# Output stage of a transformer layer: raw weights requested in the gate's stage, other first PSUM banks, form buffers held for six jobs, high parts of a set ahead of its low parts

## The chip, the cores and the metric

The kernel runs on one core of a Trainium2 chip. TensorE (PE in the profile) multiplies, VectorE (DVE) and ScalarE (ACT) do the elementwise work, GpSimd (POOL) and SyncE (SP) issue DMA transfers between the chip's main memory and the core's SBUF. Matmul results land in PSUM, which has eight banks of 128 x 512 fp32. The metric is the device time of one execution, in microseconds (us).

## The reference

One layer with 512 tokens and a width of 2048, everything in fp32:

```python
def reference(x, ...):                       # kind 0 for the one layer here
    h = rms_norm(x, norm_g[i, 0])
    y = gla_mixer(h, gla_w_in, gla_w_a2, gla_b_a, gla_g_norm, gla_w_out)
    x = x + y
    x = x + swiglu(rms_norm(x, norm_g[i, 1]), ffn_w_gu[i], ffn_w_down[i])
    return x

def gla_mixer(h, w_in, w_a2, b_a, g_norm, w_out):
    q, k, v, r, a_lr = split(h @ w_in)
    ...                                      # gated linear attention in chunks of 64 tokens -> o
    o = rms_norm(o, g_norm) * silu(r)        # the gate
    return o @ w_out                         # the output product

def swiglu(h, w_gu, w_down):
    g, u = jnp.split(h @ w_gu, 2, axis=-1)
    return (silu(g) * u) @ w_down
```

## The kernel before, in words

**fp32 by halves.** TensorE multiplies in a reduced form of fp32 (fp32r). Each operand is split in a high part (a cast on ACT) and a low part (the operand less its high part, on DVE), and a product is three matmuls: high x high, high x low, low x high. So each raw weight block that comes by DMA passes ACT (`hi`, L121 or L697) and DVE (`lo`, L122 or L698) before PE can use it. A ring of three pairs (`wp`, bufs=3) holds the parts.

**The gate's stage.** The last of the products with w_in are four groups (`group(X, KT)`), one for each head of the gate; each multiplies 16 blocks and leaves its sums in four banks named `acc`. The raw blocks come by SP (L108) into two buffers. `gate(h, banks)` (L575) then takes a group's banks: four products acc x R1 (L579) into `t`, a Silu on ACT (L583), a product with the attention's output (L584), and after that its pieces in steps, spread over the work that follows by a queue. `put` splits each piece into high and low parts (`split_into`, L559) and stores them through POOL to a DRAM tensor gF; `load_form` (L573) loads them back on SP as "forms", the left operands of the next products.

**The output stage and the FFN in jobs.** Each big product is done by a scheme of seven products of blocks in place of eight. A "group" is 28 jobs: seven phases (`PHASES`) of four chunks. Groups 0 and 1 are the two halves of the product with w_out, the groups from 2 on are w_gu's and w_down's. A job is twelve 128x512 matmuls (`run_job`, L1064 to L1066). Ahead of job m, `add_stage(m + 3)` subtracts or adds raw blocks on DVE (L688) where the phase wants a sum of blocks, and `split_stage` makes the parts (L697, L698) up to two jobs ahead. `load` (L676) asks for raw blocks on SP. The sums of the phases stand in pairs of banks x, y and z. The first pairs are made in `first_banks`, out of the same eight banks that acc (five) and the attention's `mis` (three) held before.

**What is hung on job numbers.** `at(m, fn)` runs fn behind job m's matmuls in program order. After each phase of groups 0 and 1, `take_out` moves the banks into SBUF pieces u, v, s, w (L883 copies, L886 to L898 adds), adds the residual x, and `finish` squares a finished piece on ACT for the second norm (L875) and stores it to x1d (L876, POOL). In group 0, `make_forms` turns the finished pieces (transposes, L766) and makes the FFN's forms in four steps, each in one job: `one` (high and low parts times the gain, L565 on ACT and L566 on DVE, and a scaled copy, L795), `two` (store of `hh` and `hl`, and sums on DVE, L789), `three` (parts of the sums, L824 and L825), `four` (store of the rest). The stores go to xF by POOL (L803). There are four such sets, and `hh`, `hl` and `hs` have one buffer each. Group 1's forms are made by a class `Direct` straight into place. `second_norm` (L743) computes the inverse root of the row sums: DVE, then two table functions on ACT (L162, L163), then a Newton step on DVE (L164 to L167).

The program's order on each engine is the order in which the code issues it; nothing is rescheduled. What sets the order around the change is the job numbers in `at`, the place of the calls of `load`, and the steps of `gate`.

Of the kernel before, what the change touches and what calls it, by code (L numbers as in the profile page):

```python
# [14 lines left out]
P = 128  # L15
# [21 lines left out]
def f32(ap):  # L37
    return ap.bitcast(F32)
# [3 lines left out]
def trunk_kernel(ctx: ExitStack, tc: tile.TileContext, x, xT, cst, masks, wa2r, w_in, w_out, w_gu, w_down, out):  # L42
# [516 lines left out]

    def split_into(hi, lo, src, g=None):  # L560
        if g is None:
            nc.scalar.copy(hi, src)  # L562
            nc.vector.tensor_sub(lo, src, f32(hi))
        else:
            nc.scalar.activation(hi, src, AF.Copy, scale=g)  # L565
            nc.vector.scalar_tensor_tensor(lo, src, g, f32(hi), ALU.mult, ALU.subtract)  # L566
# [69 lines left out]
    for h in range(3):  # L636
        queue.append(gate(h, banks))
        tick()
        banks = group(X, KT, after=early_load) if h == 2 else group(X, KT)
    while queue:  # L640
        tick()
    for f in ("e0", "e1", "e2", "e3"):
        load_form(gF, f, 2)
    x1d = dram.tile([P, 4, D], F32, name="x1d")

# [63 lines left out]
    for blk in range(3):  # L709
        for j in range(4):  # L710
            load(0, blk, j)
# [13 lines left out]
    first_banks = {q: [bank(f"q{pr}{i}") for i in range(2)] for q, pr in (("z", 0), ("y", 1), ("x", 2))}  # L725
# [18 lines left out]
    def second_norm():  # L744
        z = sp.tile([P, S], F32, tag="u1", name="z")
        c = z[:, 16:20]
# [4 lines left out]
        rsqrt(c, D, r2c, (z[:, 0:4], z[:, 8:12]))  # L751

    at(first_of[G0, 1] + 2, second_norm)
# [43 lines left out]
    def make_forms(dst, c, i, tiles, m, banks, g=None):  # L797
# [7 lines left out]
        def one():  # L805
# [4 lines left out]
            if g is None:  # L810
                split_into(hi[:, 0:2], lo[:, 0:2], a1)
                split_into(hi[:, 2], lo[:, 2], a2[:, 1])
            else:
                for k, src in enumerate((a1[:, 0], a1[:, 1], a2[:, 1])):
                    split_into(hi[:, k], lo[:, k], src, g[min(k, 1)])
            copy_scaled(sm[:, 0], a2[:, 0], g)
# [17 lines left out]
    class Direct:  # L834
# [16 lines left out]
        def pure(self, f, i):  # L851
            t, (a1, a2), g = self.place(f), self.a[i], self.gain(i)
            src, gg = {"e0": (a1[:, 0], g[0]), "e3": (a1[:, 1], g[1]), "l2": (a2[:, 1], g[1])}[f]
            split_into(t[:, 0, i], t[:, 1, i], src, gg)
# [7 lines left out]
        def part(self, f, i):  # L862
            t = self.place(f)
            split_into(t[:, 0, i], t[:, 1, i], self.sm[i][:, ("e1", "e2", "l0", "l1").index(f)])


    def take_out(g, ph, XYZ, keep):
# [6 lines left out]
        def finish(tt, nb, t, junk):  # L874
            nc.scalar.activation(junk, t, AF.Square, accum_out=ssq2[:, 4 * tt + nb : 4 * tt + nb + 1])  # L875
            nc.gpsimd.dma_start(x1d[:, tt, nb * G : (nb + 1) * G], t)  # L876

        for i in range(2):
# [6 lines left out]
            elif ph == 3:  # L885
                nc.vector.tensor_add(keep["u", i], keep["u", i], y)  # L886
                finish(i, 2 * p + 1, keep["u", i], y)
            elif ph == 4:
                nc.vector.tensor_add(keep["v", i], keep["v", i], b)
                finish(2 + i, 2 * p + 1, keep["v", i], y)  # L890
                t = keep["x", i] = piece()
                nc.sync.dma_start(t, x_at(2 + i, 2 * p))
            elif ph == 5:
                nc.vector.tensor_add(keep["s", i], keep["s", i], z)
                finish(i, 2 * p, keep["s", i], z)
            else:
                t = keep["w", i] = sp.tile([P, S], F32, tag=f"v{i}", name="w")
                nc.vector.tensor_add(t, keep["x", i], b)  # L898
                finish(2 + i, 2 * p, t, b)
        if ph == 4:  # L900
            tiles = [keep[k, i] for k in "uv" for i in range(2)]
            c = 2 * p + 1
            if p == 0:
                g_ = [[g2[:, 4 * c + k : 4 * c + k + 1] for k in (i, 2 + i)] for i in range(2)]
                at(m0 + 21, lambda: make_forms(xF, c, 0, tiles, m0 + 21, tb_pair(), g_[0]))
                at(m0 + 22, lambda: make_forms(xF, c, 1, tiles, m0 + 25, pair(1), g_[1]))
            else:
                d = Direct(c)
                at(m0 + 21, lambda: d.turn(tiles, 0, tb_pair()))
                at(m0 + 22, lambda: (d.turn(tiles, 1, pair(1)), d.pure("e0", 0)))  # L910
                at(m0 + 23, lambda: (d.pure("e0", 1), d.sums(0)))
                at(m0 + 24, lambda: [d.part(f, 0) for f in ("e1", "e2", "l0", "l1")])
                at(m0 + 25, lambda: d.sums(1))
                at(m0 + 26, lambda: [d.part(f, 1) for f in ("e1", "e2", "l0", "l1")])
# [231 lines left out]
```

## Time and profile before

| | us |
|---|---|
| median of 3 runs | 2108.28 (2108.11 to 2109.48) |
| the profiled execution | 2110.94 |
| its span in the profile | 2109.1 |
| PE busy | 2073.3 (98%) |
| DVE busy | 1604.6 (76%) |
| ACT busy | 938.1 (44%) |
| POOL busy | 311.4 (15%) |

PE's mean granted clock over the span is 0.994. The output stage lies between about 630 and 857 us of the span: group 0 from 637.9 to 720.6, group 1 to about 818, then the first w_gu group. Each row of a timeline has a start, a length, engine, line, operation, output and inputs; in brackets stands the time for which the engine was idle just before, and what released it.

### The profile page before, as it was taken

What the parts mean: (1) busy time and instruction counts of PE and PEld (TensorE: products, weight loads), DVE (VectorE), ACT (ScalarE), POOL (GpSimd) and SP (SyncE); (2) the same over time, 40 slices, a digit from 0 to 9 for tenths busy, and PEclk for the clock granted to TensorE, in tenths of its full rate; (3) what the DMA queues carried; (4) which work ended last, traced back from release to release, by engine and by line L of the source; (5) the groups of instructions that cost most, each with busy time, mean ns of one, the idle gap of its engine ahead of it and who ended that gap; (6) DMA issues with size and microseconds to landing.
All of it is one profiled execution on the core that took longest, in us unless ns stands there. A gap on an engine that the chain in (4) does not pass through costs nothing.

```text
span 2109.1 us, 24558 instructions
## 1 busy us (share of the span) xinstructions
PE 2073.3 (98%) x9314; PEld 1714.5 (81%) x9314; DVE 1604.6 (76%) x1778; ACT 938.1 (44%) x1165; POOL 311.4 (15%) x315
## 2 busy tenths in 40 slices
PE   9999999999998989999999999999999999999999
PEld 7887888888877767788888888888888888888887
DVE  7857475755448778788788788788798787888887
ACT  6343433333334445554454454454455454333333
POOL 5315151422111120010010010010010010000000
PEclk9999999999999999999999999999999999999999
DMA  6222222225586866444644644644645776675642
GB/s 209 80 81 71 70 83 77 71 85 165 161 307 200 310 201 258 141 138 146 185 136 139 185 141 134 186 148 125 195 146 164 249 274 239 219 254 192 233 145 100
DMA packets 161333, 350.22 MB, mean 166 GB/s; under 512 B 14400, under 2 KB 30912, under 8 KB 161216
## 3 DMA queue, kind: packets, MB, share of 16 engines
q1 hardware_dynamic: 136704, 274.76, 40.4%
q0 software_dynamic: 21440, 71.84, 10.0%
q10 hardware_dynamic: 3072, 2.06, 0.3%
q8 instruction: 73, 1.20, 0.2%
q14 instruction: 44, 0.36, 0.1%
HBM read 279.93 MB, written 68.68 MB: 165 GB/s over the span
## 4 chain that ended last, share of the span: by engine, by line
PE 86%; issue 6%; DVE 4%; POOL 2%; DMA 1%; ACT 1%; SPq 0%; POOLq 0%; ACTq 0%; DVEq 0%
PE bank L1066 20%; PE bank L1065 20%; PE bank L1064 20%; PE acc L134 7%; PE acc L133 7%; PE acc L135 7%; PE mis L427 2%; PE bank L766 1%; DVE lo L698 1%; PE mis L485 1%; DVE raw L688 0%; PE mis L133 0%; PE mis L135 0%; PE mis L134 0%; DVE qt L392 0%
## 5 line engine op out<-in xcount | busy, mean ns | idle before, releaser
L697 ACT CAST hi<-raw 128x1024 fp32r<-128x1024 f32 x518 | 543.7, 1053 | 629.1 <-PE bank L1066 538.0
L698 DVE TENSOR_TENSOR lo<-raw,hi 128x1024 fp32r<-128x1024 f32 x518 | 631.3, 1223 | 216.0 <-ACT hi L697 205.5
L1064 PE MATMUL bank<-hi,fe 128*128 128x512 f32 x1184 | 466.9, 394 | 14.5 <-ACT hi L697 7.2
L1065 PE MATMUL bank<-lo,fe 128*128 128x512 f32 x1184 | 465.2, 393 | 6.9 <-DVE lo L698 6.9
L1066 PE MATMUL bank<-hi,fe 128*128 128x512 f32 x1184 | 464.3, 392 | 1.0 <-DVE fe L566 1.0
L688 DVE TENSOR_TENSOR raw<-raw 128x1024 f32<-128x1024 f32 x296 | 361.2, 1220 | 5.5 <-DMA raw<-w_out 2.7
L1064 PE MATMUL bank<-hi,fl 128*128 128x512 f32 x888 | 345.9, 390 | 0.3 <-DMA fl<-gF 0.3
L1065 PE MATMUL bank<-lo,fl 128*128 128x512 f32 x888 | 345.8, 389 | 0.0
L1066 PE MATMUL bank<-hi,fl 128*128 128x512 f32 x888 | 345.5, 389 | 0.0
L1064 PEld LDWEIGHTS bank<-hi,fe 128*128 128x128 f32 x1184 | 224.1, 189 | 62.5 <-ACT hi L697 9.0
L1065 PEld LDWEIGHTS bank<-lo,fe 128*128 128x128 f32 x1184 | 224.1, 189 | 57.8 <-DVE lo L698 12.0
L1066 PEld LDWEIGHTS bank<-hi,fe 128*128 128x128 f32 x1184 | 223.8, 189 | 48.2 <-DVE fe L566 1.4
L122 DVE TENSOR_TENSOR lo<-raw,hi 128x1024 fp32r<-128x1024 f32 (+1 forms) x97 | 123.8, 1285 | 163.4 <-ACT hi L121 150.7
L133 PE MATMUL acc<-x,hi 128*128 128x512 f32 x512 | 202.9, 396 | 1.7 <-ACT x L170 1.2
L134 PE MATMUL acc<-x,hi 128*128 128x512 f32 x512 | 199.6, 390 | 0.3 <-DVE x L171 0.3
L135 PE MATMUL acc<-x,lo 128*128 128x512 f32 x512 | 199.6, 390 | 0.1
L1065 PEld LDWEIGHTS bank<-lo,fl 128*128 128x128 f32 x888 | 166.7, 188 | 35.9 <-DVE lo L698 0.2
L1064 PEld LDWEIGHTS bank<-hi,fl 128*128 128x128 f32 x888 | 166.6, 188 | 35.8 <-issue 1.0
L1066 PEld LDWEIGHTS bank<-hi,fl 128*128 128x128 f32 x888 | 166.7, 188 | 34.3
L121 ACT CAST hi<-raw 128x1024 fp32r<-128x1024 f32 (+1 forms) x97 | 100.6, 1040 | 206.1 <-PE acc L134 140.5
L803 POOL DMA_DIRECT2D hF<-hh x44 | 33.0, 750 | 785.8 <-ACT hh L562 685.2
L133 PEld LDWEIGHTS acc<-x,hi 128*128 128x128 f32 x512 | 96.2, 188 | 22.6 <-ACT x L170 1.5
(208 smaller groups left out, 2101.2 us busy)
## 6 DMA issues: line engine op xcount, KB each, us to landing
raw<-w_gu SPq DMA_DIRECT2D x176, 512.0 KB, 4.4
raw<-w_down SPq DMA_DIRECT2D x88, 512.0 KB, 5.6
raw<-w_in SPq DMA_DIRECT2D x64, 512.0 KB, 3.9
fe<-hF SPq DMA_DIRECT2D x44, 512.0 KB, 5.7
fl<-hF SPq DMA_DIRECT2D x33, 512.0 KB, 6.7
raw<-w_out SPq DMA_DIRECT2D x32, 512.0 KB, 9.3
raw<-w_in SPq DMA_DIRECT2D x62, 256.0 KB, 3.2
gF<-st POOLq DMA_DIRECT2D x48, 256.0 KB, 4.8
```

Of the source, the lines that this page charges most:

```text
L121: nc.scalar.copy(hi[:, c], raw[:, c])
L122: nc.vector.tensor_sub(lo[:, c], raw[:, c], f32(hi[:, c]))
L133: nc.tensor.matmul(out, ah, bh, start=start, stop=False)
L134: nc.tensor.matmul(out, ah, bl, start=False, stop=False)
L135: nc.tensor.matmul(out, al, bh, start=False, stop=stop)
L427: nc.tensor.matmul(bk[:, g * w : (g + 1) * w], kt[:, c, gg * P : (gg + 1) * P], qt[:, o : o + w], start=c == 0, stop=c == 1,)
L688: (nc.vector.tensor_add if ph == 5 else nc.vector.tensor_sub)(to, a, b)
L697: nc.scalar.copy(hi, raw)
L698: nc.vector.tensor_sub(lo, raw, f32(hi))
L1064: nc.tensor.matmul(o, ah, bh, start=a and begin, stop=False, skip_group_check=True)
L1065: nc.tensor.matmul(o, ah, bl, start=False, stop=False, skip_group_check=True)
L1066: nc.tensor.matmul(o, al, bh, start=False, stop=z, skip_group_check=True)
```

## The change

1. The twelve raw w_out blocks that group 0 needs first are asked for in the loop over the gate's groups, six after the first and six after the second of the three groups in it, ahead of the following w_in blocks on SP. Before, they were asked for behind all w_in blocks and the forms.
2. `first_banks`: z and y are made, then the two banks "tb", then x. So x, the first pair that is used, lies on the two banks where before "tb" lay, which belonged to `mis` and not to `acc`.
3. The four sets of `make_forms` begin at the offsets 21, 27, 33, 39 of group 0 in place of 21, 25, 29, 33 (each step `one` a job behind). Loads of the forms from xF go from the offsets 13, 14, 15, 16, 18, 22, 26 of group 1 to 18, 18, 19, 19, 20, 22, 26.
4. `split_all` casts all high parts of a set on ACT, makes the scaled copy behind them, and then all low parts on DVE, where `split_into` alternated piece by piece.
5. `finish` is postponed to fixed jobs (offsets 17, 21, 25, 31), and w's Square writes its junk to the x piece in place of the bank.
6. `second_norm` is cut in three steps over three jobs, of which the first lies a job earlier than before.

The matmuls and their order are the same.

```diff
@@ split_into becomes split_all
+    def split_all(parts, then=lambda: None):
+        for hi, _, src, g in parts:
+            if g is None:
+                nc.scalar.copy(hi, src)
+            else:
+                nc.scalar.activation(hi, src, AF.Copy, scale=g)
+        then()
+        for hi, lo, src, g in parts:
+            if g is None:
+                nc.vector.tensor_sub(lo, src, f32(hi))
+            else:
+                nc.vector.scalar_tensor_tensor(lo, src, g, f32(hi), ALU.mult, ALU.subtract)
...
@@ the gate's loop, which now stands behind load()'s definition
     for h in range(3):
         queue.append(gate(h, banks))
         tick()
         banks = group(X, KT, after=early_load) if h == 2 else group(X, KT)
+        if h < 2:
+            for blk in range(3):
+                for j in range(2 * h, 2 * h + 2):
+                    load(0, blk, j)
...
-    for blk in range(3):
-        for j in range(4):
-            load(0, blk, j)
     split_stage(0)
     split_stage(1)
     add_stage(4), add_stage(5)
...
-    first_banks = {q: [bank(f"q{pr}{i}") for i in range(2)] for q, pr in (("z", 0), ("y", 1), ("x", 2))}
+    first_banks = {q: [bank(f"q{pr}{i}") for i in range(2)] for q, pr in (("z", 0), ("y", 1))}
+    bank("tb", 2), bank("tb", 2)
+    first_banks["x"] = [bank(f"q2{i}") for i in range(2)]
...
@@ second_norm(m): the first step at m; root on ACT, newton on DVE
+        at(m + 1, root)
+        at(m + 2, newton)
+
+    at(first_of[G0, 1] + 1, lambda: second_norm(first_of[G0, 1] + 1))
...
@@ make_forms, one()
+            split_all(parts, lambda: copy_scaled(sm[:, 0], a2[:, 0], g))
...
@@ take_out
+        def finish(tt, nb, t, junk, m):
+            def later():
+                nc.scalar.activation(junk, t, AF.Square, accum_out=ssq2[:, 4 * tt + nb : 4 * tt + nb + 1])
+                nc.gpsimd.dma_start(x1d[:, tt, nb * G : (nb + 1) * G], t)
+
+            at(m0 + m, later)
...
-                at(m0 + 22, lambda: make_forms(xF, c, 1, tiles, m0 + 25, pair(1), g_[1]))
+                at(m0 + 22, lambda: make_forms(xF, c, 1, tiles, m0 + 27, pair(1), g_[1]))
...
-                at(m0 + 29, lambda: make_forms(xF, c, 0, tiles, m0 + 29, tb_pair(), g_[0]))
-                at(m0 + 30, lambda: make_forms(xF, c, 1, tiles, m0 + 33, pair(banks_of[2]), g_[1]))
+                at(m0 + 29, lambda: make_forms(xF, c, 0, tiles, m0 + 33, tb_pair(), g_[0]))
+                at(m0 + 30, lambda: make_forms(xF, c, 1, tiles, m0 + 39, pair(banks_of[2]), g_[1]))
...
-        for ph, k in enumerate((13, 14, 15, 16, 18, 22, 26)):
+        for ph, k in enumerate((18, 18, 19, 19, 20, 22, 26)):
```

How it moves the instructions, at three places. First SP's queue through the gate's stage into the output stage (`raw<-w_in` are the gate's blocks, `raw<-w_out` the output product's, `fe<-gF` forms). Before:

```order
L108 DMA raw<-w_in 128x2x512 x37
L573 DMA fe<-gF_3251 128x1024 x2
L108 DMA raw<-w_in 128x2x512
L573 DMA fe<-gF_3251 128x1024 x2
L108 DMA raw<-w_in 128x2x512
L573 DMA fe<-gF_3252 128x1024 x2
L573 DMA fe<-gF_3253 128x1024 x4
L676 DMA raw<-w_out 128x2x512 x12
```

and with the change:

```order
L108 DMA raw<-w_in 128x2x512 x28
L675 DMA raw<-w_out 128x2x512 x6
L108 DMA raw<-w_in 128x2x512 x8
L675 DMA raw<-w_out 128x2x512 x6
L108 DMA raw<-w_in 128x2x512
L582 DMA fe<-gF_3251 128x1024 x2
L582 DMA fe<-gF_3253 128x1024 x4
```

(Some rows in which a block of w_in and two forms alternate are left out.) The two batches of six stand ahead of the last twelve w_in blocks and of all forms; before, the twelve stood behind them.

Second the first matmuls of the output stage on PE, with the semaphores that they wait for. Before:

```order
L135 MATMUL acc_4226<-x_423,lo_4437 128x512
L1064 MATMUL bank_4576<-hi_4545,fe_4269 128x512 [waits DMAHW6_49,DVE_49,Activation_49]
L1065 MATMUL bank_4576<-lo_4546,fe_4269 128x512
L1066 MATMUL bank_4576<-hi_4545,fe_4269 128x512
L1064 MATMUL bank_4577<-hi_4545,fe_4269 128x512 [waits PE_49]
```

and with the change:

```order
L135 MATMUL acc_4250<-x_423,lo_4461 128x512
L1096 MATMUL bank_4578<-hi_4545,fe_4293 128x512 [waits DMAHW2_49,Activation_49]
L1097 MATMUL bank_4578<-lo_4546,fe_4293 128x512 [waits DVE_49]
L1098 MATMUL bank_4578<-hi_4545,fe_4293 128x512
L1096 MATMUL bank_4579<-hi_4545,fe_4293 128x512 [waits PE_49]
```

The first matmul no longer waits for DVE; the second, which uses the low part, does.

Third ACT from group 0's fifth phase into group 1: the high parts `hh` (L565, now L566), the scaled copy `hs` (L795, now L820), the parts of the sums (L824, now L847) of the sets, and the Squares `ssq_71` of `finish` (L875, now L905). Before:

```order
L875 ACTIVATE bank,ssq_71<-v 128x512 x2
L697 CAST hi<-raw 128x1024 x2
L565 ACTIVATE hh<-bank,c_sb 128x256 x3
L795 ACTIVATE hs<-bank,c_sb 128x256
L697 CAST hi<-raw 128x1024 x2
L824 CAST hh<-hs 128x1024
L875 ACTIVATE bank,ssq_71<-s 128x512 x2
L697 CAST hi<-raw 128x1024 x2
L565 ACTIVATE hh<-bank,c_sb 128x256 x3
```

and with the change:

```order
L905 ACTIVATE bank,ssq_71<-v 128x512 x2
L696 CAST hi<-raw 128x1024
L566 ACTIVATE hh<-bank,c_sb 128x256 x3
L820 ACTIVATE hs<-bank,c_sb 128x256
L696 CAST hi<-raw 128x1024 x2
L847 CAST hh<-hs 128x1024
L696 CAST hi<-raw 128x1024
L905 ACTIVATE bank,ssq_71<-s 128x512 x2
L696 CAST hi<-raw 128x1024 x3
L566 ACTIVATE hh<-bank,c_sb 128x256 x3
```

Between the parts of one set's sums and the next set's first high parts lie four high parts of weights in place of two.

## Rows read from the trace of the kernel before

**Rows 1.** The page: the span, and its first part, busy us of each engine with the share of the span and the instructions.

```profile
span 2109.1 us, 24558 instructions
PE 2073.3 (98%) x9314; PEld 1714.5 (81%) x9314; DVE 1604.6 (76%) x1778; ACT 938.1 (44%) x1165; POOL 311.4 (15%) x315
```

**Rows 2.** Busy time by stretch: from and to, length, then PE, PE's weight loads, DVE, ACT and POOL busy (instructions), PE's granted clock, DMA share, GB/s. The gate's last group; a stretch at the output stage's start; two in the stretch of the form sets; one near the second norm; group 2's start.

```profile
587.00:630.50 43.50, 43.50 (x193) 35.83 (x191) 20.06 (x24) 13.34 (x18) 7.53 (x14) 1.00 0.90 334
632.70:642.95 10.25, 5.08 (x12) 4.04 (x13) 8.74 (x12) 2.90 (x5) 0.00 (x0) 0.50 1.03 373
728.28:731.69 3.41, 3.17 (x8) 2.49 (x9) 3.30 (x7) 1.04 (x1) 0.00 (x0) 0.50 0.28 97
762.41:765.82 3.41, 3.41 (x9) 2.65 (x9) 3.30 (x6) 1.76 (x3) 0.00 (x0) 0.50 0.14 48
851.16:854.57 3.41, 3.41 (x10) 2.62 (x9) 3.41 (x6) 1.54 (x3) 0.00 (x0) 0.50 0.00 0
818.00:857.00 39.00, 34.80 (x148) 27.06 (x148) 36.19 (x56) 23.05 (x40) 1.08 (x2) 0.96 0.18 69
```

**Rows 3.** The timeline of PE: the first matmul of the output stage, and the first wait for a low part in it.

```profile
637.87 0.77 PE L1064 MATMUL bank<-hi,fe 128*128 128x512 f32 x1 [7.21 <-ACT t L583]
...
657.70 0.50 PE L1065 MATMUL bank<-lo,fe 128*128 128x512 f32 x1 [0.56 <-DVE lo L698]
```

**Rows 4.** The waits of PE and of ACT in 700 to 775 us: line, waited for, us in total, times, longest us.

```profile
PE bank L1064 <- ACT hi L697: 6.5, 2, 3.8
PE bank L1065 <- DVE lo L698: 4.1, 6, 1.2
PE bank L766 <- DVE w L898: 0.5, 2, 0.3
...
ACT hh L565 <- DMA xF<-hh: 13.3, 3, 5.7
...
ACT hh L565 <- DVE hl L566: 3.0, 4, 1.3
ACT hs L795 <- DVE hl L566: 2.3, 4, 0.6
```

**Rows 5.** The waits of PE in 775 to 870 us, columns as in rows 4.

```profile
PE bank L1065 <- DVE lo L698: 2.2, 2, 1.7
PE bank L1066 <- DVE fe L566: 1.0, 1, 1.0
PE bank L1064 <- ACT hi L697: 0.7, 1, 0.7
PE bank L766 <- DVE w L898: 0.2, 1, 0.2
```

**Rows 6.** The view of line L676 in 600 to 640 us: its loads on SP (duration in ns, first and last start), and the time from issue to landing.

```profile
L676 SPq DMA_DIRECT2D raw<-w_out x12: 368/518/885, 620.2 to 630.9; - x12
...
DMA to landing us min/median/max: 6.5/11.8/12.1
```

**Rows 7.** The timeline of ACT around the end of the gate's stage: the first three high parts of w_out.

```profile
626.88 1.05 ACT L697 CAST hi<-raw 128x1024 fp32r<-128x1024 f32 x1 [7.93 <-DMA raw<-w_out]
628.44 1.05 ACT L697 CAST hi<-raw 128x1024 fp32r<-128x1024 f32 x1 [0.51 <-DMA raw<-w_out]
630.47 1.04 ACT L697 CAST hi<-raw 128x1024 fp32r<-128x1024 f32 x1 [0.98 <-PE acc L134]
```

**Rows 8.** The timeline of DVE, from the second low part of w_out to job 6.

```profile
629.53 1.23 DVE L698 TENSOR_TENSOR lo<-raw,hi 128x1024 fp32r<-128x1024 f32 x1 [0.34 <-ACT hi L697]
633.45 2.52 DVE L688 TENSOR_TENSOR raw<-raw 128x1024 f32<-128x1024 f32 x2 [2.70 <-DMA raw<-w_out]
635.89 2.48 DVE L579 TENSOR_TENSOR t<-acc,R 128x512 f32<-128x512 f32 x4
...
656.43 1.22 DVE L698 TENSOR_TENSOR lo<-raw,hi 128x1024 fp32r<-128x1024 f32 x1
...
658.16 1.22 DVE L688 TENSOR_TENSOR raw<-raw 128x1024 f32<-128x1024 f32 x1
659.30 1.22 DVE L698 TENSOR_TENSOR lo<-raw,hi 128x1024 fp32r<-128x1024 f32 x1
```

**Rows 9.** The timeline of SP in the gate's stage: two issues of w_in blocks.

```profile
540.33 8.60 SPq L108 DMA_DIRECT2D raw<-w_in  x2
...
548.56 43.89 SPq L108 DMA_DIRECT2D raw<-w_in  x9
```

**Rows 10.** A store of the first set on POOL, and the ACT row that its landing released (second set).

```profile
715.81 0.76 POOL L803 DMA_DIRECT2D xF<-hh  x1
...
723.36 0.47 ACT L565 ACTIVATE hh<-bank,c_sb 128x256 fp32r<-128x256 f32 x1 [5.72 <-DMA xF<-hh]
```

**Rows 11.** The timeline of DVE in the first set.

```profile
705.89 0.88 DVE L566 SCALAR_TENSOR_TENSOR hl<-bank,c_sb,hh 128x256 fp32r<-128x256 f32 x2 [0.54 <-ACT hh L565]
...
709.39 2.04 DVE L789 SCALAR_TENSOR_TENSOR hs<-bank,c_sb,hs 128x256 f32<-128x256 f32 x4
...
712.55 1.23 DVE L825 TENSOR_TENSOR hs<-hs,hh 128x1024 fp32r<-128x1024 f32 x1
```

**Rows 12.** The timeline of DVE: a low part, and the first Newton row of the second norm.

```profile
826.06 1.23 DVE L698 TENSOR_TENSOR lo<-raw,hi 128x1024 fp32r<-128x1024 f32 x1 [0.61 <-ACT hi L697]
...
846.47 0.16 DVE L164 TENSOR_TENSOR z<-r2c 128x4 f32<-128x4 f32 x1 [1.79 <-ACT r2c L163]
```

More of the change, by code (lines that the diff above doesn't have):

```diff
@@ L635, in trunk_kernel @@
     st = mid.enter_context(tc.tile_pool(name="st", bufs=7, reuse_waits="tile"))
[L636 to L644, printed above, removed]
     groups = [(w_out, range(4), (2 * p * G, (2 * p + 1) * G)) for p in range(2)]
@@ L707, in split_stage @@
                     load(g + 1, ph - 4, k)
-    for blk in range(3):
-        for j in range(4):
-            load(0, blk, j)
+    for h in range(3):
+        queue.append(gate(h, banks))
+        tick()
+        banks = group(X, KT, after=early_load) if h == 2 else group(X, KT)
+        if h < 2:
+            for blk in range(3):
+                for j in range(2 * h, 2 * h + 2):
+                    load(0, blk, j)
+    while queue:
+        tick()
+    for f in ("e0", "e1", "e2", "e3"):
+        load_form(gF, f, 2)
+    x1d = dram.tile([P, 4, D], F32, name="x1d")
     split_stage(0)
@@ L750, in second_norm, with root, newton @@
             nc.vector.tensor_add(c, c, v[:, :, n])
-        rsqrt(c, D, r2c, (z[:, 0:4], z[:, 8:12]))
-    at(first_of[G0, 1] + 2, second_norm)
+        nc.vector.tensor_scalar(a, c, 1.0 / D, EPS, ALU.mult, ALU.add)
+        def root():
+            nc.scalar.activation(t, a, AF.Ln)
+            nc.scalar.activation(r2c, t, AF.Exp, scale=-0.5)
+        def newton():
+            nc.vector.tensor_mul(t, r2c, r2c)
+            nc.vector.tensor_mul(t, t, a)
+            nc.vector.tensor_scalar(t, t, -0.5, 1.5, ALU.mult, ALU.add)
+            nc.vector.tensor_mul(r2c, r2c, t)
+        at(m + 1, root)
+        at(m + 2, newton)
+    at(first_of[G0, 1] + 1, lambda: second_norm(first_of[G0, 1] + 1))
     xF = [dram.tile([P, 7, 2, 2, 256], F32, name=f"xF{c}") for c in range(2)]
@@ L849, in place, with pure @@
             return self.t[f]
[L851 to L854, printed above, removed]
+        def pure(self, *which):
+            parts = []
+            for f, i in which:
+                t, (a1, a2), g = self.place(f), self.a[i], self.gain(i)
+                src, gg = {"e0": (a1[:, 0], g[0]), "e3": (a1[:, 1], g[1]), "l2": (a2[:, 1], g[1])}[f]
+                parts.append((t[:, 0, i], t[:, 1, i], src, gg))
+            split_all(parts)
         def sums(self, i):
@@ L860, in sums, with part @@
             sums(sm, *self.a[i], self.gain(i))
-        def part(self, f, i):
-            t = self.place(f)
-            split_into(t[:, 0, i], t[:, 1, i], self.sm[i][:, ("e1", "e2", "l0", "l1").index(f)])
+        def part(self, *which):
+            parts = []
+            for f, i in which:
+                t = self.place(f)
+                parts.append((t[:, 0, i], t[:, 1, i], self.sm[i][:, ("e1", "e2", "l0", "l1").index(f)], None))
+            split_all(parts)
     def take_out(g, ph, XYZ, keep):
@@ L898, in take_out @@
                 nc.vector.tensor_add(t, keep["x", i], b)
-                finish(2 + i, 2 * p, t, b)
+                finish(2 + i, 2 * p, t, keep["x", i], 31)
         if ph == 4:
@@ L909, in take_out @@
                 at(m0 + 21, lambda: d.turn(tiles, 0, tb_pair()))
[L910 to L912 removed]
+                at(m0 + 22, lambda: (d.turn(tiles, 1, pair(1)), d.pure(("e0", 0))))
+                at(m0 + 23, lambda: (d.pure(("e0", 1)), d.sums(0)))
+                at(m0 + 24, lambda: d.part(*[(f, 0) for f in ("e1", "e2", "l0", "l1")]))
                 at(m0 + 25, lambda: d.sums(1))
[L914 to L916 removed]
+                at(m0 + 26, lambda: d.part(*[(f, 1) for f in ("e1", "e2", "l0", "l1")]))
+                at(m0 + 27, lambda: d.pure(("e3", 0), ("e3", 1)))
+                at(m0 + 28, lambda: d.pure(("l2", 0), ("l2", 1)))
         if ph == 6:
```

35 lines of the change are left out of this document (11 added, 24 removed).

## The prediction

> **What bounds the kernel now.** I read the page first [rows 1]: TensorE (PE) is busy 2073.3 us of a span of 2109.1. No matmul is added or removed, so only what PE loses can be won: its waits and the stretches in which it runs at the lower of its two clock levels. The list of clocks by windows shows both rates [rows 2]. At a granted clock of 1.00 (2.4 GHz) the 192 matmuls of the gate stage's last group (the row counts 193) take 43.50 us, 0.227 us each, so that a job of twelve takes 2.72 us. At 0.50 (1.2 GHz) twelve took 5.08 us. Before that window PE had stood still for 7.21 us [rows 3]; the other three windows at 0.50 lie in stretches with many waits. There I count half of PE's busy time as lost.
>
> Then I read PE's waits by stretch, then for each the timeline of the engine that it waits for. The output stage (630 to 857 us) holds nearly all that the change touches, in three places:
> - Its start: PE waits 7.21 us for ACT before the first job and 0.56 for a low part at 657.70 [rows 3], and twelve matmuls run at half clock: 5.08 - 12 x 0.227 = 2.4 us lost [rows 2]. Together 10.2.
> - The four sets of forms (700 to 775): waits of 6.5 + 4.1 + 0.5 = 11.1 us [rows 4], and two half-clock windows with 3.17 and 3.41 us busy, half of which is 3.3 [rows 2]. Together 14.4.
> - The end of group 1 and the second norm (775 to 870): waits of 2.2 + 1.0 + 0.7 + 0.2 = 4.1 us [rows 5], and half of 3.41 us [rows 2] is 1.7. Together 5.8.
>
> All three are 30.4 us: no more can be won here.
>
> **Part 1, early raw loads and other first banks.** Before, the twelve raw w_out loads leave SP from 620.2 to 630.9, behind all w_in loads and forms, and take 6.5 to 12.1 us to land [rows 6]. ACT stood 7.93 us for the first and 0.51 for the second [rows 7], DVE 2.70 for the blocks that it subtracts (L688) [rows 8]. Only then came the four products acc x R1 (L579, at 635.89), and the first matmul of the stage, which takes over acc's banks, waited for them; PE's row names ACT's L583, but its list of semaphores in the order has DVE's in it, and now has not. With the raw blocks there and banks 6 and 7 free, PE need not stop at all: 7.2 + 2.4 = 9.6 us go.
>
> But DVE then sets the pace. Around the wait at 657.70 DVE's low parts stand without an idle time before them [rows 8], while the gate's work runs between them. So PE wins over jobs 3 to 9 what DVE's chain wins. I build that chain: the third high part got its slot in the ring at 630.47 [rows 7], the one before it a unit of two blocks earlier, 24 x 0.227 = 5.44 us, at 625.03. Before, from the start of that high part (628.44) to the end of its low part (629.53 + 1.23 = 630.76) it took 2.32 us; now that ends at 627.35. The pair L688 (2.52) follows to 629.9, and L579 starts there, not at 635.89: 6.0 us earlier. I take **6.0 us**. Ends: 9.6, if DVE catches up by itself, and 4.5, if the new waits of PE (10.2 - 6.0 = 4.2) are followed by another half-clock window, for which rows 2 have 1.5 to 1.7.
>
> The loads themselves I cost at nothing. A batch is 6 x 512 KB = 3.1 MB; at the 373 GB/s of the window at the stage's start [rows 2] that is 8.4 us. SP's issues of w_in at 540.33 and 548.56 stand 8.2 us apart [rows 9], and the next block that waits is needed late: two raw buffers and three pairs of high and low parts lie ahead of PE, of which I count four units of 5.44 us, 22 us. If that cover is gone, PE stands still in the gate's stage (below).
>
> **Part 2, the sets of forms.** A set is made on ACT and DVE, stored by POOL, and the next needs its buffers. Before, ACT waited for the stores' landing three times, 13.3 us in all [rows 4]; the longest, 5.72, ended at 723.36 for a store issued at 715.81, so 7.5 us [rows 10], and PE stood 3.8 us behind it [rows 4]. ACT's wait of 5.72 cost PE 3.8, so some 2 us of such a wait are covered by the high parts ahead. Now the sets are six jobs apart, and between the store and the next set lie three jobs (8.2 us) in place of one: the 7.5 us fit, with 0.7 to spare and 2 us more covered. The Square and the x1d stores that stood ahead of the sets' own move behind them. ACT's waits for DVE's low part of the same bank (3.0 + 2.3 us [rows 4]) go with the new order of the parts. So the 6.5 and 0.5 go, and both half-clock windows.
>
> PE's wait for low parts (4.1) does not go entirely. A set costs DVE 3 x 0.46 + 2.04 + 1.23 = 4.6 us [rows 11]. A job with a sum costs it 2.28 us of PE's 2.72 (two passes of 1.14, the distance of 658.16 and 659.30 in rows 8), 0.44 free, or 2.7 in six jobs; one without a sum leaves 1.6. Sets 0 and 1 fall in jobs whose next phases have no sum; sets 2 and 3 fall in phases 1 to 3 of group 1, and each overruns by some 1.9 us. DVE's lead of two jobs takes in part of these 3.8. I leave 1.6 us of waits, between 0.2 (the lead takes in nearly all) and 4.1 (nothing changes for DVE). Gain 14.4 - 1.6 = **12.8 us**; ends 14.2 and 10.3, or 7.0 if 4.1 remain and both windows too.
>
> **Part 3, the second norm and the last forms.** DVE was the busiest here, 36.19 of 39 us [rows 2]. It waited 0.61 at 826.06 and 1.79 at 846.47 for ACT [rows 12], the latter inside the norm; both go, since root and Newton step now lie in different jobs and the parts are grouped: 2.4 us less of DVE's time. Of PE's 4.1 I leave 2.3 (4.1 - 2.4 = 1.7 if each microsecond counts, 4.1 if none does), and take the half-clock window as gone with the rest. Gain 5.8 - 2.3 = **3.5 us**; ends 4.1 and 0.
>
> Moved at no cost: x's loads and the loads of forms (18 to 20 instead of 13 to 16 jobs into group 1), which still lie ahead of their use; the postponed Square, on an ACT that is 44% busy [rows 1]. If that cover were gone, ACT's next high part would come late by 1.5 us.
>
> **Sum.** 6.0 + 12.8 + 3.5 = 22.3 us. The profiled execution took 2110.94 us, so 2088.6 in its terms; it stands 2.66 above the median of the runs (2108.28), so **2086 us**. By the ends of the terms: 27.9 (2080) to 14.8 (2093).
>
> **The rivals.**
> - DVE catches up at the start (chance 0.10). For it: PE's one wait for a low part there was 0.56 us [rows 3]; but for that DVE kept PE's pace. Against: DVE's rows around 657 stand without an idle time [rows 8], so it has nothing in hand for an earlier PE. Term 1 is 9.6: 2082 us.
> - Set 1's buffers are still late (0.10). The margin is 0.7 us and 2 us of cover, and w_out loads took up to 12.1 us to land [rows 6]; against it: the 13.3 us are the waits with one job's distance. A store of 10.5 us, say, would bring back about 1 us of waiting, and with DVE's debt behind it and a half-clock window (1.7) and as much again in set 2, some 4 us: 2090 us. The row gives 7.5 us to such a store [rows 10]. The Trainium skill, page DMA: Bandwidth & Descriptors, section Anatomy of one DMA — SWDGE (gpsimd) path, puts a fixed 2.0 us and bytes at 436 GB/s to a DMA from this queue: by it, an estimate of 3.2 us for 512 KB, this rival would have no chance and the sum would stay. The trace disagrees by more than a factor of two, so the rival keeps its chance.
> - DVE sets the pace throughout (0.10). For it: DVE is busy 36.19 of 39 us [rows 2]. Low parts then cost PE the same 4.1 us in the sets, with both half-clock windows: term 2 is 7.0; term 3 is 1, term 1 is 4.5, in sum 12.5: 2096 us.
> - No change (0.04): what is won at the three places comes back as other waits in group 1: 2106 us. Against: PE has no other long wait to fall into.
> - **Slower** (0.04): the w_out loads hold up w_in on the same queue. It decides when a batch of six takes more than some 24 us (a gap of 8.2 and 16 of the 22 us ahead), a rate under 130 GB/s; at 75 GB/s each batch lasts 42 us, PE stands 18 us twice and loses about 3.4 at half clock, 39 in all, more than the 22.3 won: 2125 us. Against: 334 to 373 GB/s in the windows at 587 and 632 [rows 2].
>
> That the change does not do what it says is excluded by the order: the first matmul has lost its wait for DVE.
>
> **How the numbers follow.** The forecast has 0.62. Its own range is 2080 to 2093. The first two rivals (2082, 2090) lie inside it. DVE's case (2096) is taken in, and 2 us below for the doubt in the bounds: 2078 to 2097 should hold 8 in 10. Faster by over 0.2% (4.2 us, about what a measurement can tell from no change): all but the last two cases, 0.92; within it 0.04; slower 0.04.
>
> **What would show it.** Right: no wait of PE at the first w_out matmul and full clock behind it; L579 some 6 us earlier against the end of the gate's last group, with about 4 us of waits for low parts in jobs 3 to 9; no wait of ACT on a landing xF store over 2 us; no half-clock window in 720 to 775 and 850 to 855; DVE's wait for r2c gone. Wrong: a wait of PE for a high part in the gate's stage, new half-clock windows, or waits for low parts over 10 us in the output stage.

## The result, and the profile after

| | us |
|---|---|
| changed kernel, median of 4 runs | 2080.64 (2079.27 to 2081.84) |
| kernel before, median of 4 runs | 2108.88 (2108.11 to 2111.17) |
| ratio | 0.9864, 95% interval 0.9847 to 0.9881 |
| profiled execution, its span | 2081.49, 2079.7 |

The change wins 28.2 us. The forecast was 2086, 22.3 us won, in a range of 2078 to 2097: right in sign and inside the range, at its lower end. The page of the changed kernel, for [rows 1]:

```profile
span 2079.7 us, 24526 instructions
PE 2065.5 (99%) x9314; PEld 1713.0 (82%) x9314; DVE 1601.7 (77%) x1778; ACT 938.7 (45%) x1165; POOL 313.5 (15%) x315
```

PE's waits in the changed kernel, in 600 to 660, 700 to 775 and 775 to 870 us, for [rows 4, 5] and the 7.21 us of [rows 3]; these three rows are all the waits that the list still has in the output stage:

```profile
PE bank L1097 <- DVE lo L697: 1.6, 1, 1.6
...
PE bank L1097 <- DVE lo L697: 0.3, 1, 0.3
...
PE bank L1097 <- DVE lo L697: 0.7, 1, 0.7
```

Three stretches of it, columns as in [rows 2]: the start, the form sets, the second norm.

```profile
630.00:668.00 38.00, 36.20 (x150) 28.95 (x149) 35.61 (x41) 20.41 (x27) 6.89 (x10) 0.96 0.29 72
720.00:775.00 55.00, 54.65 (x245) 44.67 (x244) 53.49 (x61) 32.06 (x46) 16.26 (x22) 1.00 0.72 225
818.00:857.00 39.00, 39.00 (x170) 31.26 (x169) 35.97 (x45) 22.26 (x31) 0.00 (x0) 1.00 0.47 138
```

PE is busy for 54.65 of 55 us in the sets, and DVE for 53.49: DVE is nearly full there, and PE yet hardly waits.

To see where the time went I took the same matmul, counted from the first on PE, in each two traces, and compared the starts. Won against the profile of the kernel before by the matmul that there starts at the time in the heading (the state at 540 us, which differs by up to 2.4 us through the stages ahead, taken off):

| kernel | 661 | 720 | 775 | 857 | 2104 |
|---|---|---|---|---|---|
| changed | 6.6 | 7.7 | 24.1 | 29.9 | 30.0 |
| changed, profiled again | 7.2 | 7.4 | 23.9 | 29.8 | 30.3 |

So the start won 7.4 to 7.7 us, the sets 16.4, and the stretch around the second norm 5.8. The two profiles of the changed kernel differ by up to 0.6 us in a column, so less than that between two kernels says nothing.

### The profile page after: what moved, and what is told of

It reads as the page before. It is cut to its first block, busy times and chain, and to the rows that moved or that the text cites. A ratio compares the mean times of both kernels' runs of the same rounds, so it can differ in the third digit from the quotient of the medians.

```text
span 2079.7 us, 24526 instructions
## 1 busy us (share of the span) xinstructions
PE 2065.5 (99%) x9314; PEld 1713.0 (82%) x9314; DVE 1601.7 (77%) x1778; ACT 938.7 (45%) x1165; POOL 313.5 (15%) x315
## 4 chain that ended last, share of the span: by engine, by line
PE 94%; DVE 4%; ACT 1%; POOL 0%; issue 0%; DMA 0%; SPq 0%; DVEq 0%; ACTq 0%; POOLq 0%
PE bank L1097 22%; PE bank L1098 22%; PE bank L1096 22%; PE acc L134 8%; PE acc L133 8%; PE acc L135 7%; PE mis L427 2%; PE bank L791 1%; DVE lo L697 1%; DVE raw L687 1%; PE mis L485 1%; PE mis L135 0%; PE mis L133 0%; PE mis L134 0%; DVE qt L392 0%
```

## The experiments

Their gains by the same matmuls, from the profile of each:

| kernel | 661 | 720 | 775 | 857 | 2104 | ratio to before |
|---|---|---|---|---|---|---|
| only_loads | 7.2 | 7.8 | 7.0 | 7.0 | 8.1 | 0.9967 (0.9956 to 0.9979) |
| only_banks | 0.1 | 1.0 | 0.5 | 2.1 | 2.0 | 0.9996 (0.9986 to 1.0005) |
| only_spacing | 0.1 | 0.5 | 13.9 | 12.2 | 12.2 | 0.9949 (0.9933 to 0.9965) |
| only_split | 0.2 | 1.0 | 2.3 | 1.0 | 1.4 | 0.9996 (0.9986 to 1.0005) |
| no_split | 7.2 | 7.9 | 22.6 | 26.7 | 27.1 | 0.9886 (0.9869 to 0.9902) |
| no_finish | 7.2 | 8.0 | 21.6 | 25.5 | 26.1 | 0.9885 (0.9871 to 0.9900) |
| no_norm | 7.2 | 7.3 | 23.7 | 25.9 | 25.9 | 0.9890 (0.9875 to 0.9904) |
| defer_low | 6.8 | 6.9 | 23.3 | 29.1 | 29.3 | 0.9871 (0.9856 to 0.9886) |
| no_banks | 7.2 | 8.1 | 24.5 | 30.3 | 30.1 | 0.9850 (0.9835 to 0.9865) |
| pool_sums | 7.2 | 7.8 | 24.3 | 30.1 | 31.1 | 0.9855 (0.9839 to 0.9871) |
| pool_defer | 5.7 | 5.9 | 22.3 | 28.2 | 28.7 | 0.9864 (0.9849 to 0.9879) |

They ran in three sets, each beside the kernel before on the same chip, whose median was 2108.80 in the first (only_loads to only_split), 2107.88 in the second (no_split to defer_low) and 2111.32 in the third; ratios are compared, not medians of different sets. The ratios of no_split, no_finish and no_norm lie 0.002 to 0.003 above the changed kernel's, with intervals that overlap with its own (0.9847 to 0.9881): what these three lose is read from the columns, one profile each. By 857 us the four parts run alone won 22.3 us together, of the whole change's 29.9; the postponed Squares and the divided second norm were not run alone.

**only_loads.** The change with everything undone but this:

```diff
+        if h < 2:
+            for blk in range(3):
+                for j in range(2 * h, 2 * h + 2):
+                    load(0, blk, j)
...
-    for blk in range(3):
-        for j in range(4):
-            load(0, blk, j)
```

> The kernel before with one part of the change: the twelve raw w_out loads asked for in the gate's loop; banks 4 and 5 are still the first. Theory A (DVE's chain is the cause: late raw blocks hold up L688, this L579, and this PE): L579 starts some 6 us earlier against the end of the gate's last group, PE's wait at the first w_out matmul falls from 7.2 us to 1 to 3 us, and from there on nearly all of the 7 us that the whole change wins by 661 us is there: 4 to 6 us won, about 2104 us. Rival B (taking over acc's banks is the cause): PE's wait there stays over 5 us, at most 2 us won, about 2107 us.

Measured: 2102.23 us. PE's first matmul of the stage, in its timeline:

```profile
631.37 0.47 PE L1091 MATMUL bank<-hi,fe 128*128 128x512 f32 x1 [0.85 <-ACT hi L693]
```

A wait of 0.85 in place of 7.21 us, and 7.2 us won by job 8: theory A, with a little more than it expected. The early loads alone are the whole gain of the start.

**only_banks.** The change with everything undone but this:

```diff
+    bank("tb", 2), bank("tb", 2)
+    first_banks["x"] = [bank(f"q2{i}") for i in range(2)]
```

> The kernel before with one part of the change: the first pair x on the two banks that were tb's; the raw loads stay late. Theory A: PE starts without the 7.2 us wait, since high and low part of job 0 are there, but DVE still stands 2.7 us for the raw blocks and does L688 and L579 at 633 to 638, so the low parts of the next jobs come as late as before: PE waits for them instead, 5 us or more, and at most 2 us are won, about 2107 us. Rival B: the wait goes and nothing takes its place: 7 us or more won, about 2101 us.

Measured: 2107.32 us, no change that the interval shows. DVE, and then PE, in this kernel:

```profile
633.69 2.58 DVE L684 TENSOR_TENSOR raw<-raw 128x1024 f32<-128x1024 f32 x2 [2.44 <-DMA raw<-w_out]
636.19 2.48 DVE L585 TENSOR_TENSOR t<-acc,R 128x512 f32<-128x512 f32 x4
```

```profile
639.86 0.50 PE L1093 MATMUL bank<-lo,fe 128*128 128x512 f32 x1 [3.37 <-DVE lo L694]
```

DVE's rows stand as in [rows 8]; PE begins the stage on time, and then waits for the low parts, 6.0 us in four waits with two half-clock windows behind them. The bank that is taken over was where the wait showed, not what caused it: theory A.

**only_spacing.** The change with everything undone but this:

```diff
-                at(m0 + 22, lambda: make_forms(xF, c, 1, tiles, m0 + 25, pair(1), g_[1]))
+                at(m0 + 22, lambda: make_forms(xF, c, 1, tiles, m0 + 27, pair(1), g_[1]))
...
-                at(m0 + 30, lambda: make_forms(xF, c, 1, tiles, m0 + 33, pair(banks_of[2]), g_[1]))
+                at(m0 + 30, lambda: make_forms(xF, c, 1, tiles, m0 + 39, pair(banks_of[2]), g_[1]))
...
-        for ph, k in enumerate((13, 14, 15, 16, 18, 22, 26)):
+        for ph, k in enumerate((18, 18, 19, 19, 20, 22, 26)):
```

> The kernel before with one part of the change: form sets at offsets 21, 27, 33, 39 and the later loads from xF; order of the parts, Squares and norm as before. Theory A (ACT's wait for the stores and DVE's load are two causes): ACT's 13.3 us for landing stores fall under 2, PE's 6.5 us for high parts go and with them the half-clock windows, but of the 4.1 us for low parts 3 or more stay, since ACT and DVE still alternate on a set: 10 to 12 us won in the sets, about 2098 us. Rival B (the low parts are late only because ACT is): they go with the high parts', all of the 16.5 us between 714 and 770 are won, about 2092 us.

Measured: 2097.47 us. Its waits of ACT in 690 to 775 us, and of PE and then DVE in 700 to 775:

```profile
ACT hh L567 <- DVE hl L568: 6.7, 4, 2.6
...
ACT hh L567 <- DMA xF<-hh: 1.6, 2, 1.3
...
PE bank L1091 <- DVE lo L694: 2.8, 5, 1.2
...
DVE lo L694 <- ACT hi L693: 10.0, 7, 2.4
DVE hl L568 <- ACT hh L567: 2.7, 5, 0.5
```

The wait for the stores falls from 13.3 to 1.6 us, PE's for high parts is gone, and 2.8 of 4.1 us for low parts stay, a little under the 3 that theory A expected. In the sets 13.4 us are won by 775 us (13.9 - 0.5) and 11.6 by 800, where 10 to 12 were expected: theory A. ACT's wait for DVE's part of the bank grew from 3.0 to 6.7: with the stores out of the way, the alternation comes to the fore.

**only_split.** The change with everything undone but `split_all`, which makes the high parts, the scaled copy and then the low parts:

```diff
-                split_into(hi[:, 0:2], lo[:, 0:2], a1)
-                split_into(hi[:, 2], lo[:, 2], a2[:, 1])
+                parts = [(hi[:, 0:2], lo[:, 0:2], a1, None), (hi[:, 2], lo[:, 2], a2[:, 1], None)]
...
+            split_all(parts, lambda: copy_scaled(sm[:, 0], a2[:, 0], g))
```

> The kernel before with one part of the change: all high parts of a set ahead of its low parts. Theory A: ACT's waits of 3.0 + 2.3 us for DVE's low parts go, but ACT reaches its wait for the landing stores that much earlier, so that the waits there grow from 13.3 to 15 us or more and PE's 6.5 us stay; in 818 to 857 the 0.6 us wait of DVE goes and 1 to 2 us are won: 1 to 3 us in all, about 2107 us. Rival B (the alternation is the cause of the late parts): PE's waits for high and low parts fall by half or more: 6 us or more won, 2103 us or less.

Measured: 2107.49 us, no change that the interval shows. ACT waits 13.6 us for landing stores, so the freed time does not all reappear there (15 or more were expected), but PE still waits 5.3 us for high parts, and 1.3 us are won in the sets: theory A. Nothing is won in 818 to 857, which was wrong in its expectation.

**no_split.** The changed kernel, with the loop of `split_all` making each low part right behind its high part:

```diff
-                nc.scalar.activation(hi, src, AF.Copy, scale=g)
-        then()
-        for hi, lo, src, g in parts:
...
+                nc.scalar.activation(hi, src, AF.Copy, scale=g)
+                nc.vector.scalar_tensor_tensor(lo, src, g, f32(hi), ALU.mult, ALU.subtract)
+        then()
```

> The changed kernel with the old order of the parts: high and low alternate piece by piece. In the sets the spacing alone won 12.1 us and the whole change 16.5; this run and the next tell who wins the rest. Theory A (the order of the parts, since the spaced kernel's waits for low parts come from DVE held up by the alternation): 3 to 4 us of the rest go again in 730 to 775, and up to 2 in 800 to 860: about 2085 us, with 2 us or more of PE's waits for low parts back. Rival B (the postponed Squares win it, since ACT then stands no more behind DVE's sums of a finished piece): at most 1 us goes, 2081 to 2082 us.

Measured: 2083.20 us; the sets win 14.7 us by 775 and 12.9 by 800, against 16.4: 3.5 us lost, 1.7 of them by 775. Its waits of PE and of DVE in 700 to 775 us:

```profile
PE bank L1094 <- DVE lo L694: 2.4, 3, 1.2
...
DVE hl L568 <- ACT hh L567: 1.6, 3, 0.5
```

PE waits 2.4 us for low parts in place of 0.3, and DVE 1.6 us for the sets' high parts, for which it does not wait in the changed kernel. Theory A for the sets; again nothing hangs on it behind 800.

**no_finish.** The changed kernel, with:

```diff
-            at(m0 + m, later)
+            later()
...
-                finish(2 + i, 2 * p, t, keep["x", i], 31)
+                finish(2 + i, 2 * p, t, b, 31)
```

> The changed kernel with Square and x1d store at once behind each finished piece, w's junk in its bank as before. Theory A (order of the parts): ACT's waits of 1.9 us for the finished pieces come back, but lie under the two jobs that the high parts are ahead: at most 1.5 us lost, about 2082 us. Rival B (the Squares): 3 us or more lost in 730 to 775 or in 800 to 830, 2084 us or more, with PE waits for high parts.

Measured: 2083.67 us; 2.8 us lost in the sets and 1.9 behind them. Its ACT waits in 690 to 830 us:

```profile
ACT bank L905 <- DVE w L930: 4.2, 2, 3.0
ACT bank L905 <- DVE v L921: 4.1, 2, 2.2
ACT bank L905 <- DVE s L926: 4.1, 2, 2.1
...
ACT bank L905 <- DVE u L918: 2.1, 1, 2.1
```

ACT stands 14.5 us for finished pieces again. The size is rival B's. But PE's waits are for low parts, a form (`fe`, 1.0) and transposes (0.9), not for high parts: it is DVE that is held up, behind ACT, for which it waits 16.7 us in 690 to 830 us in place of 12.7. So the order of the parts and the postponed work of `finish` both matter, and overlap: by 800 us the spacing alone won 11.6, and 11.6 + 3.5 + 2.8 = 17.9 us, more than the 16.4 that the sets won. The run puts back three things at once (the Squares' time, the x1d stores' time, the place of w's junk) and does not tell them apart.

**no_norm.** The changed kernel, with:

```diff
-        at(m + 1, root)
-        at(m + 2, newton)
+        root()
+        newton()
...
-    at(first_of[G0, 1] + 1, lambda: second_norm(first_of[G0, 1] + 1))
+    at(first_of[G0, 1] + 2, lambda: second_norm(first_of[G0, 1] + 2))
```

> The changed kernel with the second norm in one piece at its old job. Theory A (DVE had no time in hand there, so that its 1.8 us wait for the root lands on PE): DVE's wait for r2c is back with 1.5 us or more, PE waits 1.5 to 3 us near 845 to 855 against the old scale and a half-clock window follows: 2 to 5 us lost, about 2084 us. Rival B (the grouped parts and the postponed Squares give DVE so much time that the norm's wait is covered): under 1 us lost, about 2081 us.

Measured: 2084.62 us. Its wait of DVE in 790 to 850 us and those of PE in 818 to 860, and then a window of it:

```profile
DVE z L770 <- ACT r2c L767: 1.8, 1, 1.8
...
PE bank L1097 <- DVE lo L697: 1.7, 1, 1.7
PE bank L1096 <- ACT hi L696: 0.8, 1, 0.8
```

```profile
825.47:828.89 3.42, 2.84 (x7) 2.29 (x8) 3.42 (x6) 3.06 (x6) 0.00 (x0) 0.50 0.00 0
```

DVE's wait comes back and PE's with it, and a half-clock window lies behind it: of the 5.8 us won here 3.6 go. Theory A.

**defer_low.** An attempt at the 1.55 us that PE still waits near 647. The changed kernel, where the last gate's `put` keeps the low part for the beginning of the next step:

```diff
+            nc.scalar.copy(parts[0], src)
+
+            def low():
+                nc.vector.tensor_sub(parts[1], src, f32(parts[0]))
...
+            owed.append(low)
+            if h < 3 or f == "l2":
+                pay()
```

> The changed kernel with one edit more: in the last gate (h = 3) the low part of each piece is made a step later than its high part, so that DVE does not stand 0.69 us three times for ACT's cast ahead of the low part for which PE waits 1.55 us at 647. Theory A (DVE sets the pace in jobs 0 to 6, and its idle time there is PE's): the 1.55 us wait and the half-clock window behind it (1.7 us) go, about 3 us won against the changed kernel: 2077 to 2078 us. Rival B (the low part hangs on ACT's high parts or on the raw blocks): the wait stays within 0.3 us, 2080 to 2081 us.

Measured: 2080.48 us. DVE stands 0.69 us for a gate's cast once in place of three times, but 1.64 for a high part of the weights at 639.50, and ACT stands 3.22 for DVE's difference, with another high part queued behind it:

```profile
642.69 0.63 ACT L608 CAST fe<-oT 128x512 fp32r<-128x512 f32 x1 [3.22 <-DVE oT L634]
643.22 1.04 ACT L720 CAST hi<-raw 128x1024 fp32r<-128x1024 f32 x1
```

PE waits 0.75 for that high part and twice 0.76 for low parts, and nothing is won. The time is rival B's, and so is the wait for ACT's high parts, though the one wait of 1.55 us did not stay: shorter ones took its place.

**pool_sums** and **pool_defer.** The changed kernel, and defer_low, with:

```diff
+            ve = nc.gpsimd if h == 3 else nc.vector
...
-            nc.vector.tensor_add(s1, a21, a22)
+            ve.tensor_add(s1, a21, a22)
```

and likewise for the other three sums and differences of the last gate.

> The changed kernel with four more instructions moved: the last gate's sums and differences of pieces (128x512, 0.69 us each on DVE, 2.8 us in all) run on POOL. Theory A (DVE's work is the bound at the start): PE's 2.7 us that are lost between 631 and 661 go for the most part, 2 us or more won there: 2078 to 2079 us. Rival B (the low parts hang on the chain through ACT's casts and the order of the steps, not on DVE's amount of work): the waits stay or move, under 1 us won, since POOL takes 1.4 to 1.6 us for such an instruction and the steps behind it come later: 2080 us or more.

> The kernel of defer_low with the four instructions on POOL as well. Theory A (work and idle time of DVE together): nothing is left of PE's loss at the start, about 2.7 us won there against the changed kernel: 2077 to 2078 us. Rival B (ACT's part): a wait for a high part of about 0.75 us, as in defer_low, stays: about 1 us won or less, 2080 us.

Measured: 2079.90 and 2080.80 us against 2079.87 for the changed kernel of the same set. The timeline of pool_sums, DVE and then POOL:

```profile
640.25 1.23 DVE L570 TENSOR_TENSOR fe<-s,fe 128x512 fp32r<-128x512 f32 x1 [1.83 <-ACT fe L564]
641.40 2.29 DVE L698 TENSOR_TENSOR lo<-raw,hi 128x1024 fp32r<-128x1024 f32 x1
...
648.22 2.31 DVE L698 TENSOR_TENSOR lo<-raw,hi 128x1024 fp32r<-128x1024 f32 x1
...
639.64 1.29 POOL L617 TENSOR_TENSOR oT<-oT 128x512 f32<-128x512 f32 x1
641.01 1.59 POOL L618 TENSOR_TENSOR oT<-oT,s 128x512 f32<-128x512 f32 x1
647.31 2.14 POOL L622 TENSOR_TENSOR oT<-oT 128x512 f32<-128x512 f32 x1 [4.70 <-DVE fe L570]
```

Two low parts, which take 1.22 us each elsewhere, took 2.29 and 2.31 beside a POOL instruction; DVE's busy time in 631 to 661 is 27.48 us, with four instructions fewer, against 27.61. So DVE was not relieved at all, and the two runs do not tell whether less of its work would help. That stays open.

**no_banks.** The changed kernel, with x back on the banks 4 and 5:

```diff
-    bank("tb", 2), bank("tb", 2)
-    first_banks["x"] = [bank(f"q2{i}") for i in range(2)]
```

> The changed kernel with the first pair x on banks 4 and 5 again; the raw loads stay early. In the kernel before, the early loads alone won 7.0 us by 661 us and the other banks alone 0.1. Theory A (DVE's work in jobs 0 to 9 sets the pace, so it does not matter whether PE starts at 630.5 or waits there for L588 and loses it later): PE waits 0.8 to 1.5 us at its first w_out matmul, the waits for low parts near 647 shrink by as much, and by 661 us the loss against the whole change is under 0.7 us: 2080 to 2082 us. Rival B (banks and loads win only together): PE loses 2 us or more at the start and does not win it back, 2083 us or more.

Measured: 2078.17 us. PE waits 0.85 us at its first matmul and 1.25 in place of 1.55 near 647; by 661 the gain is 7.2 us, as in after_again. Theory A: given the loads, the other banks are worth nothing. It has the lowest median of all, 1.7 us under after_again of the same set, but this is not the banks' doing as far as the profiles show: no_banks is 2.1 us ahead of after_again at 540 us already, before the output stage, and from there on the two stay within 0.8 us.

**after_again.** The changed kernel once more, in the third set.

> The changed kernel itself, for comparison on the same chip. 2080 to 2082 us. If the half-clock window behind the 1.55 us wait near 647 belongs to the change, it is there again; if it is a matter of the run, as in three other profiles with the same wait, it need not be.

Measured: 2079.87 us, ratio 0.9858 (0.9843 to 0.9873). The 1.55 us wait is there; the half-clock window behind it is not.

## Why the prediction was right, and where its sizes were off

**Part 1, the start: right.** The chain of the changed kernel on DVE:

```profile
626.69 1.23 DVE L697 TENSOR_TENSOR lo<-raw,hi 128x1024 fp32r<-128x1024 f32 x1 [3.35 <-ACT hi L696]
627.83 2.35 DVE L687 TENSOR_TENSOR raw<-raw 128x1024 f32<-128x1024 f32 x2
630.10 2.48 DVE L588 TENSOR_TENSOR t<-acc,R 128x512 f32<-128x512 f32 x4
```

The blocks are subtracted right behind the low part, and the products with R1 start 5.8 us earlier than in [rows 8], or 6.4 when the 0.58 us are counted by which this run reached 540 us later; 6.0 were forecast. Up to the end of that low part the forecast chain held to 0.01 us: 626.69 + 1.23 = 627.92, for 627.35 and the 0.58. PE begins the stage without a wait at 631.08, is 9.9 us ahead before its first wait, and gives 2.6 to 3.2 of them back by 661. It was to wait about 4 us for low parts there; 1.6 us are listed, 2.1 in after_again. The gift of 9.6 us that the first rival wanted did not come. The forecast was 6.0 for this term; 6.6 and 7.2 were measured at 661. What was wrong in it is the part of the other banks: without them PE does stop, for 0.85 us, but by 661 nothing is lost by it (no_banks). And one of the prediction's signs of being wrong, a new half-clock window, stood in the first profile behind the wait at 647.45 (see the last section).

**Part 2, the sets: right in mechanism, too small.** 12.8 us were forecast and 16.4 measured; this is the term that moves the result to the edge of the range. Two sizes in it were off.
- The loss before was taken from the waits as the trace lists them. Such an idle time counts from the modelled end of the matmul before, 0.39 us after its start, while without a wait the next one starts 0.23 us after it. In the kernel before:

```profile
722.88 0.39 PE L1065 MATMUL bank<-lo,fe 128*128 128x512 f32 x1
723.11 0.39 PE L1066 MATMUL bank<-hi,fe 128*128 128x512 f32 x1
727.26 0.51 PE L1064 MATMUL bank<-hi,fe 128*128 128x512 f32 x1 [3.76 <-ACT hi L697]
```

From 723.11 to 727.26 are 4.15 us; 4.15 - 0.23 = 3.92 were lost, not 3.76. With 0.16 us for each of the ten waits of [rows 4], 1.6 us are added. The matmul behind a wait often takes some 0.1 us more than 0.23, too, and holds of under 0.15 us are in no list. Summed from start to start, all that PE's steps in 720 to 775 us had over 0.227 us comes to 17.0 us, where 14.4 were counted. The statement that 30.4 us were the most that could be won falls with it.
- 1.6 us of waits for low parts were left, because a set asks more of DVE than six jobs leave. 0.3 are listed, and 1.0 are there from start to start. The overrun itself came, from the second set on, but the low parts' lead took in nearly all of it, as at the lower end that the prediction gave (0.2). The changed kernel, DVE and then PE, ahead of the second set's sums and behind the third set's:

```profile
719.47 1.22 DVE L697 TENSOR_TENSOR lo<-raw,hi 128x1024 fp32r<-128x1024 f32 x1
...
741.59 1.22 DVE L697 TENSOR_TENSOR lo<-raw,hi 128x1024 fp32r<-128x1024 f32 x1
```

```profile
723.74 0.39 PE L1097 MATMUL bank<-lo,fe 128*128 128x512 f32 x1
...
742.86 0.50 PE L1097 MATMUL bank<-lo,fe 128*128 128x512 f32 x1
```

The first of these low parts ends 3.05 us ahead of the matmul that uses it, the second, seven jobs later, 0.05 us ahead; DVE has no idle time listed between them. Where DVE also stands for the sets' high parts (2.7 us in only_spacing, 1.6 in no_split, none in the changed kernel), PE waits for low parts for 2.8 and 2.4 us. So what the spacing alone left went with the order of the parts and the postponed work of `finish`, which had no price of their own in the sum.

The stores' landing went as forecast: in the changed kernel the second set no longer waits, its store issued 9.5 us before ACT's use.

```profile
705.16 0.75 POOL L828 DMA_DIRECT2D xF<-hh  x1 [4.99 <-ACT hh L847]
...
714.69 1.20 ACT L566 ACTIVATE hh<-bank,c_sb 128x256 fp32r<-128x256 f32 x3
```

One wait of 1.4 us for a landing store is left in all of 690 to 775. The second rival had 0.7 us of margin; it was 2.0 against the 7.5 us of [rows 10].

**Part 3, the second norm: right in mechanism, too small.** 3.5 us were forecast, 5.8 measured. What was left came out nearly as forecast; the loss before was counted short, as in part 2. From start to start PE lost 7.3 us in 818 to 870 in the kernel before, where 5.8 were counted, and the same matmuls still lose 2.0 in the changed kernel, for 2.3 forecast. The list has only 0.7 of these 2.0. PE and then DVE in the changed kernel:

```profile
813.47 0.50 PE L1097 MATMUL bank<-lo,fe 128*128 128x512 f32 x1 [0.70 <-DVE lo L697]
...
816.41 0.50 PE L1097 MATMUL bank<-lo,fe 128*128 128x512 f32 x1
```

```profile
815.14 1.22 DVE L697 TENSOR_TENSOR lo<-raw,hi 128x1024 fp32r<-128x1024 f32 x1
```

The low part ends at 816.36, 0.05 us ahead of its matmul, and so it goes for six jobs, up to 828.19: their first matmuls with a low part start 2.94 us apart, where a job takes 2.72. DVE sets the pace there, and after the first no wait of PE is long enough to be listed. The Newton step now stands without an idle time:

```profile
821.03 1.22 DVE L697 TENSOR_TENSOR lo<-raw,hi 128x1024 fp32r<-128x1024 f32 x1
822.16 0.16 DVE L770 TENSOR_TENSOR z<-r2c 128x4 f32<-128x4 f32 x1
```

Here too the split of the cause was off: of the 2.4 us of DVE's waits, the 0.61 was put down to the order of the parts; no_split loses nothing here, while no_finish, in which w's Square comes at once, loses 1.9.

**The loads at no cost: right.** PE has no listed wait from 540 us to the end of the gate's stage, and by 630 us nothing is won or lost against the kernel before since 540, so the slower rival did not come about. The rival in which DVE sets the pace throughout came true in its premise, with DVE busy 53.49 of 55 us in the sets, but in its effect only in the six jobs from 813 us on.

**Where luck helped.** The terms of part 2 and part 3 came out above the upper ends that the prediction gave them (16.4 for 14.2, 5.8 for 4.1). With 6.0 for the start these ends give 24.3 us, or 2084. That 2080.64 still lies inside the range is owed to the 9.6 us end of part 1, which did not come: with 24.3 us and the 2 us taken off below, the range would have begun at 2082.

## What to carry to other kernels

The row that names a releaser tells where a wait came to light: here a bank looked like the cause, and freeing it only moved the wait onto the low parts until the raw blocks came earlier. Before the overrun of a busy engine is read as a wait of the next one, look how far ahead it stands: the low parts stood 3 us ahead of PE before the overrun and 0.05 us after it, and PE waited for them 0.35 us in the sets. And count a loss from start to start of the matmuls, not from the listed idle times: that was 17.0 us for 14.4 in the sets, and 7.3 for 5.8 around the second norm.

## What the runs showed of the hardware that was not expected

- DVE and POOL got in each other's way when both worked on SBUF tensors with two inputs: in pool_sums a DVE instruction of 0.69 us took 1.23 and two low parts of 1.22 took 2.29 and 2.31, 2.7 us more together, for the 2.8 us of work taken off DVE. The Trainium skill, page SBUF — State Buffer, section SBUF: two separate sides, says that the two engines share a port pair that one of them holds for a whole instruction while the other blocks. The trace agrees: 648.22 + 2.31 is 1.08 us behind the end of POOL's instruction at 649.45, and one such low part takes 1.22.
- The same wait of 1.55 us near 647 was followed by a window at a granted clock of 0.50 (1.2 GHz) in the first profile of the changed kernel, and by none in those of after_again, no_split, no_finish and no_norm. PE had done the same work ahead of it in all five, and was 9.85 us ahead of the kernel before in each when the wait began. The two windows, first profile and then after_again:

```profile
647.50:650.91 3.41, 3.41 (x8) 2.74 (x9) 3.38 (x5) 2.45 (x4) 2.38 (x3) 0.50 0.26 41
```

```profile
646.62:650.03 3.41, 3.01 (x12) 2.17 (x12) 3.38 (x4) 2.45 (x4) 2.38 (x3) 1.00 0.24 34
```

So whether the clock falls behind a single wait of this length differed between executions, and no run here shows why. What it cost was 0.6 us and not half the window: by 661 us the first profile had won 6.6 us and the four others 7.2, for in after_again PE stood for another 0.59 us at 650.22, where the first profile has no wait.
